# One output copied out of PSUM ungated, and a final norm finished token tile by token tile

## The chip, the cores and the metric

The kernel runs on one core of a Trainium2 chip. The metric is the device time of one execution in microseconds (us); three runs of the kernel before gave a median of 2188.82 us (2184.98 to 2189.14). A core has five engines that run their own instruction streams in order and wait for each other through semaphores: TensorE (PE; PEld is its weight load) multiplies matrices into PSUM, VectorE (DVE), ScalarE (ACT) and GpSimd (POOL) work element by element, and SyncE (SP) issues transfers between device memory and the on-chip SBUF.

## The reference, cut to what matters

One layer of a decoder takes 1024 prompt tokens and 8 x 4 sample tokens (1056 columns here) through two token mixers, retention and latent attention (MLA), and merges them. What the change touches is the end of the layer and the last norm:

```
h_ret  = retention_out(ret_o, rg, ret_gn_w) @ w_down_ret
h_mla  = (mla_o * silu(mg)) @ w_down_mla
merged = sigmoid(ga) * h_ret + sigmoid(gb) * h_mla
x = x + merged @ w_out
x = x + sigmoid(x @ w_ple_gate) * (ple @ w_ple_proj)
y = x * rsqrt(mean(x * x) + eps) * final_norm_w
```

The mean goes over the 1024 features of a token. All data are float32.

## The kernel before, in words

Activations lie transposed: features on the 128 partitions, the 1056 tokens in columns, cut in three thirds of 352. Each float32 product is made of three products of split operands (high by high, low by high, high by low: L266, L267, L268). The helper `gemm` runs the 8 x 3 multiplications of one third into a PSUM buffer `mm`, of which there are two, and calls a function that takes the result out (`evac`). `load_w` brings weights into a raw buffer `wr` (L246), ScalarE casts them to the high part `wh` (L247), VectorE subtracts for the low part `wl` (L199).

The last stage starts at about 1674 us. Its first part makes the gated MLA output: for each of eight output tiles f, the weights of w_down_mla are loaded, the gate logits `gb` come from device memory and get their sigmoid on ScalarE (L1402, L1403), and VectorE multiplies PSUM by the gate while it takes the result out to `M[f]` (L1417). The first tile takes the thirds in the order 2, 0, 1, since the last attention head's last third is ready first. After each tile, a tile of the gated retention output `go` is loaded and split for later (`gl`, L1386; cast `gh`, L1092; VectorE's subtraction, L199). Gate tiles live in three slots (`w4`), so the load of the fourth waits until the first is used up. Then follow w_down_ret (which adds to `M`, 16 tiles), w_out, and the last part.

The last part runs over the three thirds (`third(j, ...)`). In each, eight feature tiles f give a gate product `mm` and a projection `ac`; ScalarE makes the sigmoid (`sg`, L1526), VectorE multiplies by the projection (L1527) and adds `xr`, which GpSimd has put together from its two parts (L1523), into `yT` (L1528). Every two tiles, `turn` transposes `yT` back on TensorE so that tokens lie on partitions (token tiles of 128, 128 and 96 rows; L1502). ScalarE squares and sums the 256 columns into `ss` (L1504, with a read of its accumulator), VectorE multiplies by the norm's weight into `yn` (L1505). After the fourth quarter the norm is finished: VectorE adds the four sums of each of the three token tiles (L1533) and scales them (L233), GpSimd takes the power -1/2 of all three columns at once (L235), ScalarE and VectorE each scale half of the 1024 columns of each tile (L1539, L1540), and SP stores it (L1542; the last 32 rows are the sample tokens, L1544). The end of thirds 0 and 1 is run after the first feature tile of the next third has been issued. The framework orders each engine's instructions by the order of the code and its own estimate of when they are due; each engine runs its own list strictly in order.

## Time and profile before

| what | us |
|---|---|
| three runs, median (lowest to highest) | 2188.82 (2184.98 to 2189.14) |
| the profiled execution, its own time | 2187.65 |
| its span, from the first to the last instruction | 2185.8 |
| TensorE busy in the span | 2138.7 (98%) |
| VectorE busy | 1234.5 (56%) |
| ScalarE busy | 731.1 (33%) |
| GpSimd busy | 317.4 (15%) |

The granted TensorE clock of this execution was 0.995. Profile rows read: start, duration, engine, line of the kernel, operation, output<-input, shapes, count; in square brackets the idle time of the engine before the row and what released it. Rows of waits read: who waited, for whom, total us, times, longest. Rows of groups read: line, engine, operation, shapes, count, then busy us, mean ns of one, and idle time before with its releaser. A busy share is an average over a span whose stages differ, so what counts for an edit is which wait ends last at its place.

### The profile page before, as it was taken

To read this page: it belongs to the slowest core of one execution; us is meant where nothing else is said; L and a number is where in the kernel's file an instruction comes from. 1 tells how busy PE (TensorE), PEld (TensorE's weight loads), DVE (VectorE), ACT (ScalarE), POOL (GpSimd) and SP (SyncE) were. 2 spreads that over 40 slices of the span, in tenths; PEclk is the share of its full clock that TensorE was granted. 3 is DMA by queue.
4 is the path that set the end of the run, shared out by engine and by line. 5 is a ranking of instruction groups with operands and counts; after the bars stand their busy time and mean duration, and the time that the engine had idled before them with its cause. 6 is when DMAs were issued, how large, how long until landed. Compare 5 with 4: busy or idle time off the path is not lost.

```text
span 2185.8 us, 38552 instructions
## 1 busy us (share of the span) xinstructions
PE 2138.7 (98%) x15368; PEld 1858.5 (85%) x15368; DVE 1234.5 (56%) x2776; ACT 731.1 (33%) x1537; POOL 317.4 (15%) x511
## 2 busy tenths in 40 slices
PE   8999999999999999999999999899998999999997
PEld 7997877777777898888788887788887999999997
DVE  5424564565655356656666664778676353444465
ACT  6412322333333222221222311454556342222243
POOL 2211111111110022222121220122221000000121
PEclk9999999999999999999999999999999999999999
DMA  8447666566565321532613517110112353234243
GB/s 239 136 139 263 213 218 230 177 250 216 211 231 178 112 68 49 172 116 88 208 41 121 179 52 252 51 37 12 38 51 73 130 197 98 82 96 124 78 143 115
DMA packets 264356, 299.71 MB, mean 137 GB/s; under 512 B 26544, under 2 KB 221744, under 8 KB 260080
## 3 DMA queue, kind: packets, MB, share of 16 engines
q1 hardware_dynamic: 254960, 213.36, 31.5%
q0 software_dynamic: 9216, 83.89, 10.2%
q8 instruction: 121, 1.98, 0.4%
q14 instruction: 59, 0.48, 0.1%
HBM read 233.03 MB, written 64.17 MB: 136 GB/s over the span
## 4 chain that ended last, share of the span: by engine, by line
PE 61%; issue 4%; DVE 3%; DMA 1%; ACT 1%; POOL 1%; POOLq 0%; ACTq 0%; DVEq 0%; SPq 0%
PE mm L266 15%; PE mm L267 14%; PE mm L268 14%; PE ac L266 2%; PE ac L268 2%; PE ac L267 2%; PE mm L1302 2%; PE tr L1288 1%; PE ac L1245 1%; PE sc L652 1%; PE tr L852 1%; PE x L683 1%; PE ac L874 1%; PE ac L1246 1%; PE ac L1247 1%
## 5 line engine op out<-in xcount | busy, mean ns | idle before, releaser
L266 PE MATMUL mm<-xh,wh 128*128 128x352 f32 x1344 | 458.3, 341 | 1.0 <-ACT gev L413 0.8
L267 PE MATMUL mm<-xl,wh 128*128 128x352 f32 x1344 | 436.5, 325 | 0.0
L268 PE MATMUL mm<-xh,wl 128*128 128x352 f32 x1344 | 435.5, 324 | 0.0
L266 PEld LDWEIGHTS mm<-xh,wh 128*128 128x128 f32 x1344 | 253.1, 188 | 104.2 <-issue 86.5
L267 PEld LDWEIGHTS mm<-xl,wh 128*128 128x128 f32 x1344 | 254.3, 189 | 5.0 <-issue 2.7
L268 PEld LDWEIGHTS mm<-xh,wl 128*128 128x128 f32 x1344 | 253.9, 189 | 1.5 <-issue 1.5
L199 DVE TENSOR_TENSOR wl<-wr,wh 128x512 fp32r<-128x512 f32 (+2 forms) x251 | 168.5, 683 | 133.2 <-ACT wh L247 107.0
L247 ACT CAST wh<-wr 128x512 fp32r<-128x512 f32 x216 | 129.7, 618 | 285.0 <-PE mm L267 219.9
L648 DVE STREAM_TRANSPOSE kt<-craw 128x512 f32<-128x512 f32 x256 | 160.6, 681 | 108.3 <-PE sc L652 73.1
L413 ACT ACTIVATE gev<-mm 128x352 f32<-128x352 f32 x120 | 55.6, 464 | 233.0 <-PE mm L268 151.5
L266 PE MATMUL mm<-mh,wh 128*128 128x352 f32 x384 | 124.4, 324 | 1.8 <-DVE M L1417 1.8
L268 PE MATMUL mm<-mh,wl 128*128 128x352 f32 x384 | 124.3, 324 | 0.0
L268 PE MATMUL mm<-gh,wl 128*128 128x352 f32 x384 | 124.3, 324 | 0.0
L266 PE MATMUL mm<-gh,wh 128*128 128x352 f32 x384 | 124.3, 324 | 0.0
L267 PE MATMUL mm<-ml,wh 128*128 128x352 f32 x384 | 124.2, 324 | 0.0
L267 PE MATMUL mm<-gl,wh 128*128 128x352 f32 x384 | 124.1, 323 | 0.0
L266 PE MATMUL mm<-wv,xh 128*128 128x512 f32 x256 | 103.0, 402 | 0.0
L267 PE MATMUL mm<-wv,xh 128*128 128x512 f32 x256 | 100.9, 394 | 0.0
L268 PE MATMUL mm<-wv,xl 128*128 128x512 f32 x256 | 100.7, 393 | 0.0
L841 ACT ACTIVATE on<-ac,gb,gs 128x512 f32<-128x512 f32 (+1 forms) x36 | 28.0, 778 | 208.5 <-DVE gb L839 208.2
L652 PE MATMUL sc<-kt,q 32*32 32x512 f32 x2560 | 91.5, 600 | 0.0
L1523 POOL TENSOR_TENSOR xr<-x1h,x1l 128x352 f32<-128x352 f32 x24 | 24.4, 1039 | 406.2 <-DVE pT L199 326.1
(384 smaller groups left out, 4563.0 us busy)
## 6 DMA issues: line engine op xcount, KB each, us to landing
wr<-in_w_in_dram SPq DMA_DIRECT2D x144, 256.0 KB, 3.0
st<-in_state_ret_dram SPq DMA_DIRECT2D x32, 512.0 KB, 4.1
out_ret_sample_dram<-st SPq DMA_DIRECT2D x32, 512.0 KB, 3.7
wr<-in_w_ple_gate_dram SPq DMA_DIRECT2D x48, 256.0 KB, 2.7
gt<-gev SPq DMA_DIRECT2D x48, 176.0 KB, 1.8
gl<-go SPq DMA_DIRECT2D x16, 528.0 KB, 7.6
gate<-ga SPq DMA_DIRECT2D x16, 528.0 KB, 3.3
g<-gt SPq DMA_DIRECT2D x32, 256.0 KB, 3.1
```

Of the source, the lines that this page charges most:

```text
L199: dve.tensor_tensor(out=out, in0=src, in1=b32(hi), op=ALU.subtract)
L247: hi_by[0](hi, raw)
L266: pe.matmul(out, wh, xh, start=first, stop=False)
L267: pe.matmul(out, wh, xl, start=False, stop=False)
L268: pe.matmul(out, wl, xh, start=False, stop=last)
L413: act.activation(t, ps, func)
L648: dve.transpose(kt[:, 2 * i + s].rearrange("p (n r) -> p n r", r=32), src)
L652: pe.matmul(sc[32 * v:32 * v + 32, q, :], Q["q4"][qs_, j + v // 2, 2 * (g % 2) + v % 2, :], kt[qs_, v, :], start=n == 0, stop=n == NJ // 2 ...
L683: pe.matmul(pv[32 * v:32 * v + 32, :KL], pT[:, n, 32 * v:32 * v + 32], keys[v % 2][:, 8 * (v // 2) + n, :], start=n == 0, stop=n == 7, til ...
L841: act.activation(on[:n], po, AF.Identity, bias=nb[:n], scale=s[:n])
L1302: pe.matmul(po[:, :256], v[a][w], t[:, x, 256 * a:256 * a + 256], start=j + a + part == 0, stop=False, skip_group_check=True)
L1523: pool.tensor_tensor(out=xr, in0=b32(x1[f][0][:, sl]), in1=b32(x1[f][1][:, sl]), op=ALU.add)
```

## The change

In the first output tile (f = 0), VectorE now copies the product from PSUM to `M[0]` as it is. The gate is loaded and put through its sigmoid afterwards in the program, and GpSimd multiplies the whole 128 x 1056 tile by it in place. The other seven tiles are gated from PSUM as before.

In the last part, the sums of squares of one token tile now stand next to each other in `ss`, and in the fourth quarter each token tile gets its own mean (one VectorE multiply-and-sum over its four numbers with a tile of ones, `fours`) and its own root (one GpSimd power on one column), ahead of its `yn`. Scaling goes in the order of tiles 0, 1, 2 instead of 2, 0, 1, and is shared 448 columns to ScalarE and 576 to VectorE instead of 512 and 512.

```diff
     for f in range(8):
         w = load_w(A["w_down_mla"][0, :, f * P:(f + 1) * P], 8)
-        gb = gate(gbD, f)
         M.append(xs_("M", dt=F32))
         out = M[f]
-        run(gemm(w, ml, lambda j, ps, sl: dve.tensor_tensor(out=out[:, sl], in0=ps, in1=gb[:, sl], op=ALU.mult), 8,
-                 (2, 0, 1) if f == 0 else range(3)))
+        if f == 0:
+            run(gemm(w, ml, lambda j, ps, sl: dve.tensor_copy(out[:, sl], ps), 8, (2, 0, 1)))
+            gb = gate(gbD, f)
+            pool.tensor_tensor(out=out, in0=out, in1=gb, op=ALU.mult)
+        else:
+            gb = gate(gbD, f)
+            run(gemm(w, ml, lambda j, ps, sl: dve.tensor_tensor(out=out[:, sl], in0=ps, in1=gb[:, sl], op=ALU.mult), 8))
         gx.append(load_gated(f, xs_) if f < 7 else gated(f, xs_))
...
         ss = small(pz, "ss", 12, 2)
         pool.memset(ss, 1.0)
+        r = small(pz, "r", 3, 2)
...
                 q = xs_("sq", (P, 256), F32)
-                act.activation(q[:n], px[:n, :256], AF.Square, accum_out=ss[:n, 3 * quarter + i:3 * quarter + i + 1])
+                act.activation(q[:n], px[:n, :256], AF.Square, accum_out=ss[:n, 4 * i + quarter:4 * i + quarter + 1])
+                if quarter == 3:
+                    v, of = (small(pz, name, 4 if name == "of" else 1, 2) for name in ("v", "of"))
+                    dve.tensor_tensor_reduce(out=of, in0=ss[:, 4 * i:4 * i + 4], in1=fours, scale=1.0 / D, scalar=EPS,
+                                             op0=ALU.mult, op1=ALU.add, accum_out=v)
+                    pool.tensor_tensor(out=r[:, i:i + 1], in0=v, in1=nhalf, op=ALU.pow)
                 dve.tensor_tensor(out=yn[:n, hs], in0=px[:n, :256], in1=fnw[:n, hs], op=ALU.mult)
...
         turn(due, 3)
-        sums = small(pz, "sums", 3, 2)
-        dve.tensor_reduce(out=sums, in_=ss.rearrange("p (q i) -> p i q", i=3), axis=AX.X, op=ALU.add)
-        r = rstd_of(pz, sums, P, 1.0 / D, dve, 3)
-        for i in (2, 0, 1):
+        for i in range(3):
             (a, b, m), yn = tiles[i], Y[i]
             n = b - a
             o = xs_("o", (P, D), F32)
-            act.activation(o[:n, :512], yn[:n, :512], AF.Copy, scale=r[:n, i:i + 1])
-            dve.tensor_scalar(o[:n, 512:], yn[:n, 512:], r[:n, i:i + 1], None, op0=ALU.mult)
+            act.activation(o[:n, :448], yn[:n, :448], AF.Copy, scale=r[:n, i:i + 1])
+            dve.tensor_scalar(o[:n, 448:], yn[:n, 448:], r[:n, i:i + 1], None, op0=ALU.mult)
...
+    fours = pz.tile([P, 4], F32, name="fours")
+    pool.memset(fours, 1.0)
```

Below is what stands on the engines' lists, without times. First SP and ScalarE where the last stage begins; a row is a line of the kernel, an instruction, output<-input, the shape and a count. `gb` and `go` are the device memory of gate logits and of the retention output. SP before, up to the fourth gate, and after:

```order
L1402 DMA gate<-gb_82 128x1056
L1402 DMA gate<-gb_83 128x1056
L1402 DMA gate<-gb_84 128x1056
L1386 DMA gl<-go_102 128x1056
L1402 DMA gate<-gb_85 128x1056
L246 DMA wr<-in_w_down_mla_dram 128x4x128 x2
```

```order
L1402 DMA gate<-gb_82 128x1056
L1386 DMA gl<-go_102 128x1056
L1402 DMA gate<-gb_83 128x1056
L1402 DMA gate<-gb_84 128x1056
L246 DMA wr<-in_w_down_mla_dram 128x4x128 x2
L1402 DMA gate<-gb_85 128x1056
```

The first tile of `go` moves ahead of the second and third gates; the next weights move ahead of the fourth gate, which now waits for GpSimd's multiply to free its slot. ScalarE's list follows: its three gh casts stand between the first gate's sigmoid and the next two. VectorE at the same place, as one piece of the difference:

```order
 L199 TENSOR_TENSOR ml<-mla,mh 128x352 x2
-L1417 TENSOR_TENSOR M<-mm,gate 128x352 x2
+L1417 COPY M<-mm 128x352 x2
+L199 TENSOR_TENSOR gl<-gl,gh 128x352 x3
+L1417 COPY M<-mm 128x352
+L199 TENSOR_TENSOR wl<-wr,wh 128x512 x2
+L1422 TENSOR_TENSOR M<-mm,gate 128x352 x2
```

The two first multiplies become copies, and the third copy stands behind all three splits of `gl` (before, behind two of them). Third, VectorE where third 1 ends and third 2 is already under way (`rs_r` and `r` are the roots, `o` the scaled output). Before:

```order
L1540 TENSOR_SCALAR o<-yn,rs_r_22335 96x512
L1540 TENSOR_SCALAR o<-yn,rs_r_22335 128x512 x2
L1527 TENSOR_TENSOR sg<-sg,ac 128x352
L199 TENSOR_TENSOR wl<-wr,wh 128x512
L1528 TENSOR_TENSOR yT<-sg,xr 128x352
L199 TENSOR_TENSOR wl<-wr,wh 128x512
```

After:

```order
L1515 TENSOR_TENSOR yn<-tr,fnw 96x256
L1547 TENSOR_SCALAR o<-yn,r 128x576 x2
L1547 TENSOR_SCALAR o<-yn,r 96x576
L199 TENSOR_TENSOR wl<-wr,wh 128x512
L1537 TENSOR_TENSOR sg<-sg,ac 128x352
L199 TENSOR_TENSOR wl<-wr,wh 128x512
L1538 TENSOR_TENSOR yT<-sg,xr 128x352
```

Both splits of the weights now stand ahead of this `yT`; before, one of them did. At the end of the last third the three reductions, `yn` and scalings come in the same order as here, with nothing behind them.

## The prediction

> **What bounds the kernel now.** I read the page's list of costly groups first, then the waits of TensorE over the last 510 us (from 1676 us, where the last stage begins, to the end), because a change that lies in that stage can only win what TensorE waits for there, and what stands behind TensorE's last instruction.

> ```profile
> L266 PE MATMUL mm<-mh,wh 128*128 128x352 f32 x384 | 124.4, 324 | 1.8 <-DVE M L1417 1.8
> ...
> PE mm L266 <- DVE M L1417: 1.8, 1, 1.8
> PE tr L1502 <- DVE yT L1528: 0.8, 1, 0.8
> ```

> TensorE waits twice in the whole stage: once for a gated output (L1417) and once at the very end for yT. Everything between is TensorE at work without a gap, so other engines matter there only if they become late. The first wait, in order of time over all engines:

> ```profile
> 1677.70 0.96 DVE L199 TENSOR_TENSOR ml<-mla,mh 128x352 fp32r<-128x352 f32 x2 [0.17 <-ACT mh L1092]
> ...
> 1678.08 1.29 SPq L1402 DMA_DIRECT2D gate<-gb  x3
> 1679.41 0.43 SPq L1386 DMA_DIRECT2D gl<-go  x1
> ...
> 1681.74 1.28 ACT L1403 ACT_TABLE_LOAD   x1 [3.68 <-issue]
> 1682.58 0.32 PE L268 MATMUL mm<-mh,wl 128*128 128x352 f32 x1
> 1683.03 2.21 ACT L1403 ACTIVATE gate<-gate 128x1056 f32<-128x1056 f32 x2
> 1684.15 0.96 DVE L1417 TENSOR_TENSOR M<-mm,gate 128x352 f32<-128x352 f32 x2 [5.48 <-ACT gate L1403]
> 1684.72 0.43 PE L266 MATMUL mm<-mh,wh 128*128 128x352 f32 x1 [1.82 <-DVE M L1417]
> 1684.99 0.32 PE L267 MATMUL mm<-ml,wh 128*128 128x352 f32 x1
> ```

> The gate is asked for at 1678.08, its sigmoid starts at 1683.03, and VectorE, idle for 5.48 us, can multiply only at 1684.15. Two PSUM buffers (mm) are full by then, so the third block of columns cannot start.

> The end of the program, and the rate at which its last stores move:

> ```profile
> 2175.13 0.19 ACT L1504 ACTIVATION_READ_ACCUMULATOR sq<-tr 128x1 f32 x1
> 2175.35 1.14 DVE L1505 TENSOR_TENSOR yn<-tr,fnw 128x256 f32<-128x256 f32 x3 [0.33 <-ACT sq L1504]
> ...
> 2176.41 0.15 DVE L1533 TENSOR_REDUCE sums<-ss 128x3 f32<-128x12 f32 x1
> 2176.60 0.17 DVE L233 TENSOR_SCALAR rs_v<-sums 128x3 f32<-128x3 f32 x1
> 2176.85 0.86 POOL L235 TENSOR_TENSOR rs_r<-rs_v,cst 128x3 f32<-128x3 f32 x1 [25.66 <-DVE rs_v L233]
> 2177.74 1.27 DVE L1540 TENSOR_SCALAR o<-yn,rs_r 96x512 f32<-96x512 f32 x3 [0.97 <-POOL rs_r L235]
> 2177.74 1.95 ACT L1539 ACTIVATE o<-yn,rs_r 96x512 f32<-96x512 f32 x3 [1.70 <-POOL rs_r L235]
> 2178.49 0.53 SPq L1542 DMA_DIRECT2D out_y_prompt_dram<-o  x1
> 2179.07 0.58 SPq L1544 DMA_DIRECT2D out_y_sample_dram<-o  x1
> 2179.75 1.02 SPq L1542 DMA_DIRECT2D out_y_prompt_dram<-o  x2
> ```

> Here nothing overlaps: sum, root (0.86 on GpSimd), scaling, store. In the table of stretches the last three columns are clock, DMA share and GB/s:

> ```profile
> 2178.00:2179.50 1.50, 0.00 (x0) 0.00 (x0) 1.02 (x3) 1.50 (x3) 0.00 (x0) 0.50 0.00 0
> 2179.50:2181.00 1.50, 0.00 (x0) 0.00 (x0) 0.00 (x0) 0.19 (x1) 0.00 (x0) 0.50 0.87 178
> 2181.00:2183.90 2.90, 0.00 (x0) 0.00 (x0) 0.00 (x0) 0.00 (x0) 0.00 (x0) 0.50 1.00 404
> 2183.90:2185.80 1.90, 0.00 (x0) 0.00 (x0) 0.00 (x0) 0.00 (x0) 0.00 (x0) 0.50 0.01 2
> ```

> The bytes start 1.0 us after the first store's issue (2178.49 to 2179.50), crawl at 178 GB/s while the 64-row and 32-row stores go first, then run at 404; 1.9 us of completion follow.

> **The change part by part.**

> *First output copied out ungated.* The copy needs only the product in PSUM. For its length I take the multiply's, 0.96/2 = 0.48 us, which reads the same block of PSUM (a bare copy could be shorter; both lie hidden). VectorE is free at 1678.66 (1677.70 + 0.96), so the first copy is done by about 1679.3 and the first buffer is empty 3 us before the third block wants it. TensorE then goes on at the spacing of its neighbours, 0.16 us: its next start is 1682.74 instead of 1684.72, 1.98 us earlier, and the start after it comes at 1682.90 instead of 1684.99. **Term 1: -2.1 us.** The lower bound is 1.8, the wait alone.

> What is moved or added must stay hidden. The transfer of go's first tile and ScalarE's three gh casts now come before the second and third gates, and VectorE's third copy stands behind three gl splits that wait for these casts. Each of the four transfers is 528 KB; the rows below show the casts start at 1686.75, when it was the last of four, so as second of four it lands earlier; at the latest the casts start as they did.

> ```profile
> 1686.75 1.26 ACT L1092 CAST gh<-gl 128x352 fp32r<-128x352 f32 x3 [0.20 <-DMA gl<-go]
> 1688.75 1.14 ACT L247 CAST wh<-wr 128x512 fp32r<-128x512 f32 x2 [0.74 <-PE mm L267]
> 1693.13 1.08 ACT L1403 ACTIVATE gate<-gate 128x1056 f32<-128x1056 f32 x1 [3.23 <-DMA gate<-gb]
> ...
> 1700.39 1.14 ACT L247 CAST wh<-wr 128x512 fp32r<-128x512 f32 x2 [2.85 <-PE mm L267]
> ```

> At that latest the splits end near 1688.6 and the third copy at 1689.1. A block lasts 24 x 0.16 = 3.9 us, so TensorE wants this buffer at 1682.7 + 3.9 + 3.9 = 1690.5. Cover: 1.4 us at worst, price 0.

> The GpSimd multiply is 128x1056, three blocks of the size of xr, whose row (next fence) has three in 3.12 us: 3.1 us, about 1687.3 to 1690.4. Behind it waits the transfer of the fourth gate on SP's queue, and behind that the next go tile and the later weights. That gate's sigmoid ran at 1693.13; its first use is the first block of the fourth output tile. Output tiles follow at 11.64 us (1688.75 to 1700.39), so that is at about 1713. Even 3 us later it is hidden; so are the weights, which ScalarE took at 1700.39 only when TensorE let go of the slot.

> *Root, scaling and store tile by tile, at the two inner boundaries between thirds.* There TensorE already works on the next third:

> ```profile
> 2141.69 3.12 POOL L1523 TENSOR_TENSOR xr<-x1h,x1l 128x352 f32<-128x352 f32 x3
> 2141.76 3.34 DVE L1540 TENSOR_SCALAR o<-yn,rs_r 96x512 f32<-96x512 f32 x3 [0.98 <-POOL rs_r L235]
> ...
> 2145.46 0.68 DVE L199 TENSOR_TENSOR wl<-wr,wh 128x512 fp32r<-128x512 f32 x1
> 2146.06 0.51 DVE L1528 TENSOR_TENSOR yT<-sg,xr 128x352 f32<-128x352 f32 x1
> ...
> 2147.00 0.82 PE L1502 MATMUL tr<-cst,yT 128*128 128x128 f32 x6
> ```

> This yT ends at 2146.57 and is transposed at 2147.00: 0.43 us of slack. The scalings take 3.34 us beside GpSimd's xr, and 1.27 alone at the end of the program. In the changed order they start sooner (no sums, no wait for one root: 2141.25 by the steps of the next part, 0.5 earlier), but are 576 columns wide instead of 512 (3.34 x 576/512 = 3.76, 0.4 longer), and one weight split (0.60 to the next start) stands before this yT that stood behind it. The net is 0.5 us later against 0.43 of slack: a stall of 0.1 at each boundary, between 0 (the first scaling runs before xr starts) and 0.4 (the new reductions at their upper price). **Term 2: +0.2 us** (0 to 0.8).

> [...]

> *The same step at the end.* The new reduction exists nowhere in the trace; its nearest kin are the masked maximum of the attention, its read of the accumulator, and the root on one column:

> ```profile
> L1253 DVE DVE_READ_ACCUMULATOR2_ANT mx<- 128x1 f32 x26 | 3.6, 140 | 0.0
> L1253 DVE CUSTOM_DVE_ANT_0 ac<-ac,above 128x256 f32<-128x256 f32 x3 | 1.3, 426 | 0.0
> L1253 DVE CUSTOM_DVE_ANT_0 ac<-ac,above 128x128 f32<-128x128 f32 x4 | 1.2, 300 | 0.0
> ...
> L235 POOL TENSOR_TENSOR rs_r<-rs_v,cst 128x1 f32<-128x1 f32 x18 | 9.7, 551 | 1.0
> ```

> From 256 to 128 columns the time falls 0.126 us, so four columns are about 0.18; with the read, and starts that overlap, I take 0.2 us each, and 0.44 (0.30 + 0.14) as the upper bound. VectorE from 2175.35: three reductions and three yn (1.14/3 = 0.35 to the next start) end at 2175.35 + 0.6 + 1.05 = 2177.0; the first scaling (1.27/3 = 0.42, a little more for 576 columns) is done at 2177.5. ScalarE's half is earlier: statistic at 2175.65, root 0.55, so about 2176.3, and 448 columns at some 0.62 (1.95/3 = 0.65 for 512) end by 2176.95. The first store is issued at 2177.54 instead of 2178.49: 0.95 us sooner; the others are ready at 2177.95 and 2178.4, one per SP issue (0.5). The bytes then run without the pause between issues that the 178 GB/s contain. **Term 3: -1.0 us**, between -0.2 (reductions at 0.44: VectorE 0.72 later) and -1.7 (from 2178.55 all 1.44 MB at 404 GB/s, 3.57 us, so to 2182.1 instead of 2183.85).

> [...]

> **The sum**, on the profiled execution (2187.65 us: span 2185.8 and 1.85 around it): 2187.65 - 2.1 + 0.2 - 1.0 = **2184.8 us**, 0.13% less. That execution lies 1.2 under the median of the runs, 2188.82, and inside their spread of 2184.98 to 2189.14.

> **Rivals.**

> A. *VectorE is locked out at the boundaries.* If the scalings cannot start until all three xr are over (2141.5 + 3.1 = 2144.6), and then take 3 x 0.48 = 1.4, yT follows after two splits and the gate product (0.6 + 0.43 + 0.6 + 0.5) at 2148.2, 1.2 us after TensorE asks for it; twice, that is 2.4: 2184.6 + 2.4 = 2187.0. For it: three scalings cost 3.34 against 1.27. Against it: they ended with the third xr (2145.10 and 2144.81), not 1.4 after it, and now the first starts ahead of xr. Chance 0.18.

> B. *The first stall returns one block later*, behind the casts that wait for go's transfer: decisive only from 1.4 us beyond the latest start worked out above. If it takes all of term 1 back: 2184.8 + 2.1 = 2186.9. It is also the result if the copy does not free PSUM sooner. Chance 0.08.

> C. *The stores gain their upper bound and the boundaries cost nothing*: 2187.65 - 2.1 - 1.7 = 2183.9, or 2183 if the narrow stores overlap besides. Chance 0.10.

> D. *Slower.* Three roots at a boundary queue one behind another on GpSimd with VectorE's reductions between them; ScalarE stands in order behind each, so the weight cast and the gate after it come late and TensorE waits. It decides from 1.5 us lost at each boundary beyond the slack (1.5 x 2 eats terms 1 and 3). At 2.0 each: 2184.6 + 4.0 = 2188.6. For it: ScalarE already waits 2.48 us for the root there. Against it: one-column roots take 0.55, three of them 1.65, under that same wait plus slack. Chance 0.06.

> **How the numbers follow.** The forecast has 0.58: 2184.8, on its own between 2183.5 and 2186.5 by the bounds of terms 2 and 3. Two tenths of a per cent, 4.4 us, is about what a measurement of this kernel can tell from no change. The forecast's 2.9 us lies inside that; C and the faster edge of the forecast, with the runs' spread, reach beyond it. Faster 0.27, same 0.67, slower 0.06. A and D pull the upper end to 2188.4, C and the spread the lower to 2182.0.

> **What would show it.** The list of TensorE's waits should lose M and keep yT at the end; a new wait of L1507 on yT near 2104 and 2145, beyond 0.4 us, is A or D; one on the copy near 1690 is B. The stores should begin about 3 us earlier on the span's clock, 128 rows first. I am wrong on term 3 if the first store is issued later than 2.4 us after ScalarE's first accumulator read of the last turn (2175.13 to 2177.54), and on term 1 if TensorE pauses anywhere between the first and the second output tile.

## The result, and the profile after

Eleven runs of the changed kernel have a median of 2181.50 us (2178.04 to 2185.42), eleven of the kernel before 2189.14 (2184.98 to 2196.56): a ratio of 0.9971, 95% interval 0.9961 to 0.9981. The change made the kernel faster by 0.3%. The profiled execution took 2180.01 us (span 2178.2, granted clock 0.998), 7.6 us less than the profiled one of before. The forecast was 2184.8 with a range down to 2182.0. The median lies 0.5 us below that range, the profiled execution 2.0. Of the runs told of further down, one, a twelfth of kernel e3, took 11735.3 us and is in no mean.

**Where the 7.6 us come from.** TensorE's list has the same order in both programs, so the start times of the same instruction in the two traces can be subtracted. The profile after was already 3.84 us ahead at the first gate's issue (1678.08 before, 1674.24 after), ahead of anything the change touches. It was 5.92 ahead at the second output tile, 5.88 behind both inner boundaries, and 7.56 at the end. So the change itself brings 2.1 + 0.0 + 1.7, together 3.7 us of this pair, and the other half has another source.

The waits of TensorE after the change, from 1672 us to the end; the row of M is gone:

```profile
PE tr L1507 <- DVE yT L1538: 0.8, 1, 0.8
```

The other engines around the first output tile, in order of time:

```profile
1674.24 0.34 SPq L1402 DMA_DIRECT2D gate<-gb  x1
1674.64 0.42 SPq L1386 DMA_DIRECT2D gl<-go  x1
1675.28 0.53 DVE L1417 COPY M<-mm 128x352 f32<-128x352 f32 x1 [0.45 <-PE mm L268]
1679.10 0.53 DVE L1417 COPY M<-mm 128x352 f32<-128x352 f32 x1 [3.30 <-PE mm L268]
1680.42 1.24 ACT L1092 CAST gh<-gl 128x352 fp32r<-128x352 f32 x3
1680.92 1.40 DVE L199 TENSOR_TENSOR gl<-gl,gh 128x352 fp32r<-128x352 f32 x3 [1.29 <-ACT gh L1092]
1683.00 0.53 DVE L1417 COPY M<-mm 128x352 f32<-128x352 f32 x1 [0.68 <-PE mm L268]
1683.67 2.48 POOL L1419 TENSOR_TENSOR M<-M,gate 128x1056 f32<-128x1056 f32 x1 [9.50 <-ACT gate L1403]
1684.17 3.13 DVE L199 TENSOR_TENSOR wl<-wr,wh 128x512 fp32r<-128x512 f32 x2 [0.65 <-ACT wh L247]
1694.04 1.09 ACT L1403 ACTIVATE gate<-gate 128x1056 f32<-128x1056 f32 x1 [9.38 <-DMA gate<-gb]
```

All three copies now wait for TensorE, none for a gate. GpSimd's multiply lies where nobody waits for it, and the fourth gate comes late without harm.

One inner boundary:

```profile
2092.35 2.15 POOL L1514 TENSOR_TENSOR r<-v,cst 128x1 f32<-128x1 f32 x3 [19.28 <-DVE v L1512]
2093.37 2.22 DVE L1547 TENSOR_SCALAR o<-yn,r 128x576 f32<-128x576 f32 x3
2094.30 5.98 POOL L1533 TENSOR_TENSOR xr<-x1h,x1l 128x352 f32<-128x352 f32 x5
...
2095.76 1.19 DVE L199 TENSOR_TENSOR wl<-wr,wh 128x512 fp32r<-128x512 f32 x1 [0.16 <-ACT wh L247]
...
2098.23 1.26 DVE L1538 TENSOR_TENSOR yT<-sg,xr 128x352 f32<-128x352 f32 x1
...
2099.70 0.82 PE L1507 MATMUL tr<-cst,yT 128*128 128x128 f32 x6
```

The first two scalings (0.51 and 0.52 us) are over or nearly so when GpSimd's xr begins; yT ends at 2099.49, 0.21 us before TensorE takes it. The other boundary has the same durations within 0.02 us on VectorE. The single rows also show what VectorE's instructions took beside GpSimd's, on which the forecast and rival A differ. The third scaling, the two splits and yT each begin while a piece of xr runs, and end 0.3 to 0.6 us after that piece ends (xr 2094.30 to 2095.28, scaling 2094.54 to 2095.59; xr 2097.71 to 2099.11, yT 2098.23 to 2099.49). The scaling took 1.05 us there, against 0.51 and 0.52 for the two ahead of it, and yT 1.26, against 0.52 where no xr ran (2091.68). The gate product between the splits took 0.51 us inside a piece (2096.87 to 2097.38). No row lasts through all of xr; why some take longer and this one does not was not tried.

And the end of the program, with the stretches of its stores (last two columns: DMA share, GB/s):

```profile
2169.33 0.19 ACT L1509 ACTIVATION_READ_ACCUMULATOR sq<-tr 128x1 f32 x1
...
2169.55 0.16 DVE L1512 CUSTOM_DVE_ANT_0 of<-ss,fours 128x4 f32<-128x4 f32 x1 [0.33 <-ACT sq L1509]
...
2169.64 0.42 DVE L1515 TENSOR_TENSOR yn<-tr,fnw 128x256 f32<-128x256 f32 x1
...
2169.80 2.14 POOL L1514 TENSOR_TENSOR r<-v,cst 128x1 f32<-128x1 f32 x3 [24.46 <-DVE v L1512]
...
2170.39 0.67 ACT L1546 ACTIVATE o<-yn,r 128x448 f32<-128x448 f32 x1
...
2170.81 1.69 DVE L1547 TENSOR_SCALAR o<-yn,r 128x576 f32<-128x576 f32 x3
2171.39 1.26 ACT L1546 ACTIVATE o<-yn,r 128x448 f32<-128x448 f32 x2 [0.34 <-POOL r L1514]
2171.39 1.82 SPq L1549 DMA_DIRECT2D out_y_prompt_dram<-o  x3
2173.26 0.99 SPq L1551 DMA_DIRECT2D out_y_sample_dram<-o  x1
```

```profile
2172.00:2174.73 2.73, 0.00 (x0) 0.00 (x0) 0.50 (x1) 0.65 (x2) 0.00 (x0) 0.51 0.93 377
2174.73:2176.40 1.67, 0.00 (x0) 0.00 (x0) 0.00 (x0) 0.00 (x0) 0.00 (x0) 0.50 0.94 248
2176.40:2178.20 1.80, 0.00 (x0) 0.00 (x0) 0.00 (x0) 0.00 (x0) 0.00 (x0) 0.50 0.00 0
```

The first store goes out 2.06 us after ScalarE's first accumulator read (3.36 before). The bytes start fast, at 377 GB/s, and the narrow stores come last, in the stretch at 248.

**The other half of the pair.** Of the 3.84 us upstream, 3.1 arise between 743 and 753 us. In the stretches of before and then of after, the clock is the third number from the end:

```profile
745.00:750.00 5.00, 5.00 (x25) 5.00 (x25) 1.02 (x2) 0.00 (x0) 2.58 (x14) 0.59 0.26 65
750.00:755.00 5.00, 5.00 (x25) 5.00 (x24) 0.00 (x0) 0.84 (x2) 0.46 (x4) 0.72 0.60 240
```

```profile
745.00:750.00 5.00, 5.00 (x37) 5.00 (x37) 1.02 (x2) 0.00 (x0) 3.03 (x16) 1.00 0.36 107
750.00:755.00 5.00, 5.00 (x33) 5.00 (x32) 0.69 (x1) 1.53 (x3) 0.00 (x0) 1.00 0.96 332
```

TensorE was granted half its clock from 745.94 to 752.76 us in the profile before, and ran 25 matmuls in 5 us instead of 37 and 33. A suspect stands just ahead, a run of 32 narrow matmuls (32 columns each) at the end of the page attention; f2, g1 and g2 further down try it. In before:

```profile
743.01 4.19 PE L741 MATMUL x<-out,wv 128*128 128x32 f32 x32
```

Three theories were tried. **1**: the change's own effect is about 3.9 us; the rest is half-clock stretches that come and go. **2**: any change of the program shifts these stretches. **3**: all 7.6 us belong to the change.

### The profile page after: what moved, and what is told of

Same layout as the page of the kernel before. It is cut to its first block, busy times and chain, and to the rows that moved or that the text cites. A ratio compares the mean times of both kernels' runs of the same rounds, so it can differ in the third digit from the quotient of the medians.

```text
span 2178.2 us, 38580 instructions
## 1 busy us (share of the span) xinstructions
PE 2135.6 (98%) x15368; PEld 1856.0 (85%) x15368; DVE 1237.5 (57%) x2788; ACT 729.6 (33%) x1537; POOL 324.5 (15%) x519
## 3 DMA queue, kind: packets, MB, share of 16 engines
q8 instruction: 121, 1.98, 0.4%
## 4 chain that ended last, share of the span: by engine, by line
PE 62%; DVE 3%; issue 3%; DMA 1%; ACT 1%; POOL 1%; SPq 0%; ACTq 0%; POOLq 0%; DVEq 0%
PE mm L266 15%; PE mm L267 15%; PE mm L268 15%; PE ac L266 2%; PE ac L268 2%; PE ac L267 2%; PE mm L1302 2%; PE tr L1288 1%; PE sc L652 1%; PE tr L852 1%; PE ac L1245 1%; PE x L683 1%; PE ac L874 1%; PE ac L1246 1%; PE ac L1247 1%
## 5 line engine op out<-in xcount | busy, mean ns | idle before, releaser
L266 PE MATMUL mm<-xh,wh 128*128 128x352 f32 x1344 | 457.1, 340 | 0.9 <-ACT gev L413 0.7
L267 PE MATMUL mm<-xl,wh 128*128 128x352 f32 x1344 | 435.4, 324 | 0.0
L268 PE MATMUL mm<-xh,wl 128*128 128x352 f32 x1344 | 434.4, 324 | 0.0
L266 PEld LDWEIGHTS mm<-xh,wh 128*128 128x128 f32 x1344 | 252.2, 188 | 104.1 <-issue 86.5
L267 PEld LDWEIGHTS mm<-xl,wh 128*128 128x128 f32 x1344 | 253.3, 188 | 4.9 <-issue 2.7
L268 PEld LDWEIGHTS mm<-xh,wl 128*128 128x128 f32 x1344 | 253.1, 188 | 1.5 <-issue 1.5
L199 DVE TENSOR_TENSOR wl<-wr,wh 128x512 fp32r<-128x512 f32 (+2 forms) x251 | 172.2, 698 | 129.7 <-ACT wh L247 103.6
L247 ACT CAST wh<-wr 128x512 fp32r<-128x512 f32 x216 | 129.7, 618 | 277.6 <-PE mm L267 225.1
L268 PE MATMUL mm<-gh,wl 128*128 128x352 f32 x384 | 124.3, 324 | 0.0
L268 PE MATMUL mm<-mh,wl 128*128 128x352 f32 x384 | 124.3, 324 | 0.0
L266 PE MATMUL mm<-mh,wh 128*128 128x352 f32 x384 | 124.3, 324 | 0.0
L266 PE MATMUL mm<-gh,wh 128*128 128x352 f32 x384 | 124.2, 324 | 0.0
L267 PE MATMUL mm<-ml,wh 128*128 128x352 f32 x384 | 124.2, 324 | 0.0
L267 PE MATMUL mm<-gl,wh 128*128 128x352 f32 x384 | 124.2, 323 | 0.0
L266 PE MATMUL mm<-wv,xh 128*128 128x512 f32 x256 | 103.0, 402 | 0.0
L267 PE MATMUL mm<-wv,xh 128*128 128x512 f32 x256 | 100.9, 394 | 0.0
L268 PE MATMUL mm<-wv,xl 128*128 128x512 f32 x256 | 100.7, 393 | 0.0
L1533 POOL TENSOR_TENSOR xr<-x1h,x1l 128x352 f32<-128x352 f32 x24 | 26.9, 1145 | 389.9 <-DVE pT L199 311.6
```

What stands on the lines that cost most here:

```text
L199: dve.tensor_tensor(out=out, in0=src, in1=b32(hi), op=ALU.subtract)
L247: hi_by[0](hi, raw)
L266: pe.matmul(out, wh, xh, start=first, stop=False)
L267: pe.matmul(out, wh, xl, start=False, stop=False)
L268: pe.matmul(out, wl, xh, start=False, stop=last)
L1533: pool.tensor_tensor(out=xr, in0=b32(x1[f][0][:, sl]), in1=b32(x1[f][1][:, sl]), op=ALU.add)
```

## The experiments

The runs of each of three groups share a chip and the runs of the kernel before on it. There the medians of the kernel before are 2177.45 to 2178.0, some 11 us less than in the first comparison; between the profiles of before and of e1, 7.8 of this difference arise between 305 and 727 us, in the page attention, far from the change. Means are over the runs; the error behind each is the standard error.

| kernel | runs | mean us | ratio to before (95%) |
|---|---|---|---|
| before, group e | 35 | 2177.76 ± 0.35 | |
| e1, unused tile | 11 | 2177.10 ± 0.49 | 0.9996 (0.9988 to 1.0005) |
| e2, first part | 11 | 2176.28 ± 0.54 | 0.9990 (0.9981 to 0.9999) |
| e3, second part | 11 | 2175.35 ± 0.60 | 0.9989 (0.9980 to 0.9998) |
| e4, in effect the change again | 11 | 2173.79 ± 0.45 | 0.9981 (0.9972 to 0.9990) |
| before, group f | 23 | 2178.37 ± 0.56 | |
| f1, the change again | 12 | 2173.82 ± 0.70 | 0.9981 (0.9971 to 0.9991) |
| f2, change, narrow run spread | 12 | 2171.93 ± 0.55 | 0.9974 (0.9965 to 0.9984) |
| before, group g | 16 | 2178.45 ± 0.49 | |
| g1, before, narrow run spread | 11 | 2175.20 ± 0.49 | 0.9985 (0.9976 to 0.9994) |
| g2, change, narrow run spread | 6 | 2171.74 ± 0.52 | 0.9970 (0.9958 to 0.9983) |

### e1: an unused tile

```diff
+    fours = pz.tile([P, 4], F32, name="fours")
+    pool.memset(fours, 1.0)
```

> The kernel before with one unused 128x4 tile and its memset on GpSimd, which the change also brings, and nothing else of it. Theory 1 (own effect 3.9 us; the other 3.7 of the profiled pair is a half-clock stretch behind the 32 narrow matmuls at 743 us, whose appearance is luck): time as before, 2187 to 2190, some runs 3 us lower; the profile may or may not show the stretch at 746-753. Theory 2 (any change of the program shifts the clock): 2185 or less without any of the change, clock 0.997 or 0.998 in nearly all runs. Theory 3 (all 7.6 us are the change's own): 2189, as before.

The time is that of before within its interval. Its profile has a half-clock stretch of one window (3.41 us) behind the narrow matmuls, and the first profile of the change none. So this change of the program, at least, moves nothing that can be measured, and nothing speaks for theory 2.

### e2 and e3: the two parts apart

e2 has the diff of the output tile alone, e3 that of the norm alone (with `fours`).

> The first part alone: the first output copied out ungated, gated by GpSimd later; the norm as before. Theory 1: 2.1 us below the kernel before at the same clock (1.8 if the boundary savings belong to the other part), all of it between the starts of the first output's last matmul group and the next group, near 1684. Theory 3: about half of 7.6 us.

> The second part alone: root, scaling and store by token tile, gates as before. Theory 1: 1.8 us below the kernel before at the same clock, all of it behind the last accumulator read (first store 1.3 us sooner, end 1.8 sooner). Forecast on record: 0.8 us. Theory 3: the rest of 7.6 us.

By the means, e2 takes 1.5 ± 0.6 and e3 2.4 ± 0.7 us less than before, together 3.9. The traces are sharper than the means. From the last narrow attention product (the last matmul of L1302/L1307) to the 200th matmul behind it, TensorE took 34.41, 34.48 and 34.06 us in three profiles that gate from PSUM (before, e1, and g1 below), and 32.30 to 32.44 in nine that copy (32.68 in a tenth, g2): 1.4 to 2.2 us less, **2.1 in the first pair**, as forecast (in g1 TensorE's wait for M is 1.5 us instead of 1.8 or more). From the start of the last wide matmul to the end the profiles with the old norm took 12.74 to 12.77 us (before, e1, e2, g1), those with the new norm 10.98 to 11.03 (after, e3, e4, f1, f2, g2): **1.75 us**, where the forecast had 1.0.

e3 held a surprise. Here TensorE still waits for M, and this wait, too, was followed by half the clock, so that the same 200 matmuls took 35.99 us:

```profile
1672.87 0.43 PE L266 MATMUL mm<-mh,wh 128*128 128x352 f32 x1 [1.86 <-DVE M L1417]
...
1673.97 0.49 PE L266 MATMUL mm<-mh,wh 128*128 128x352 f32 x1
```

```profile
1670.00:1673.00 3.00, 1.14 (x8) 0.85 (x7) 0.71 (x2) 2.99 (x3) 0.00 (x0) 1.00 1.01 411
1673.00:1677.00 4.00, 4.00 (x17) 4.00 (x18) 1.21 (x3) 2.35 (x5) 0.00 (x0) 0.61 0.02 7
```

That is 1.5 us which the change saves now and then on top of its 2.1: in one of the four profiles that gate from PSUM.

### e4 and f1: the change again

e4 was to break up the narrow run by steps of a supply of wide work that, as TensorE's list then showed, is used up before this place:

```diff
                 pe.matmul(po[:, h * NR:(h + 1) * NR], wv[:, c, h, :], olT[:, c, h].rearrange("p b t -> p (b t)"), start=c == 0, stop=c == 1)
+            if h % 2 == 1 and h < HM - 1:
+                next(fill, None)
+                next(fill, None)
```

> The changed kernel, with the run of 32 narrow matmuls (128x32) at 743 us broken up: after each two heads two of the wide matmul steps that otherwise follow are put in, so no stretch of narrow matmuls is longer than 0.5 us. Theory 1: no half-clock stretch near 746-753 in any run; time of the changed kernel's runs that have none there (2178 to 2181), and less spread between runs. If the narrow matmuls have nothing to do with the clock: times and spread as the changed kernel (2178 to 2185).

> The changed kernel as it is, beside the kernel before on one chip. Theory 1 (own effect 3.9 us: 2.1 at the first output, 1.8 behind the last accumulator read; the rest of the first pair's 7.6 is half-clock stretches that come and go): 3.5 to 4.2 us below before by the mean, whatever the level of the chip. Theory 3 (7.6 us are its own): 7 to 8 us below.

The order of instructions did not change, so e4 is the changed kernel once more; that expectation is void, and e4, like f1, measures the change once more, on another chip than f1. Both give 0.9981; by the means 4.0 and 4.5 us less. Neither interval reaches 7.6 us (the lower ends are 6.1 and 6.3 us). Theory 3 falls there. Both profiles do have a half-clock stretch behind the narrow run.

### f2, g1 and g2: the narrow run broken up

```diff
+    rest = gate_tiles(C_MG, mgD, range(4, 5), AF.Silu)
...
             for c in range(2):
                 pe.matmul(po[:, h * NR:(h + 1) * NR], wv[:, c, h, :], olT[:, c, h].rearrange("p b t -> p (b t)"), start=c == 0, stop=c == 1)
+            if h % 2 == 1 and h < HM - 1:
+                next(rest, None)
+                next(rest, None)
...
-    run(gate_tiles(C_MG, mgD, range(4, 5), AF.Silu))
+    run(rest)
```

> The changed kernel, with the narrow matmuls (128x32) at about 740 us broken into four groups and two wide steps (six matmuls) between the groups, taken from the 88 of the next gate tile, so that the same work is done in another order. If the narrow run causes the half-clock stretch there: none near 736-753 in its profile, mean 0.5 to 1.5 us below the changed kernel on this chip, and a smaller spread. If not: as the changed kernel.

> The kernel before with its narrow matmuls at about 743 us broken into four groups with wide steps between them. Theory 1: no half-clock stretch near 746-753; mean 1 to 2.5 us below the kernel before, as much as the same edit gave the changed kernel.

> The changed kernel with the same edit, beside the one above on the same chip: with the narrow run out of the way in both, the change's own effect. Theory 1: 3.5 to 4.2 us below the run above. Theory 3 (7.6 us are the change's own): 7 to 8 us below.

None of the three profiles has half the clock there; of the eleven with the run in one piece, seven have it. One line of stretches from f1 and one from f2, the same change on one chip:

```profile
740.00:745.00 5.00, 5.00 (x24) 5.00 (x23) 0.80 (x2) 0.00 (x0) 3.00 (x16) 0.69 0.66 234
```

```profile
738.00:743.00 5.00, 5.00 (x38) 5.00 (x37) 1.74 (x3) 1.51 (x3) 1.91 (x7) 1.00 0.24 63
```

f2 gains 1.5 us on f1 at this place.

One profile of each kernel is little, but the granted clock of every run of these groups is on record, and it says the same. It averages 0.9959 in the sixteen runs of before in group g, and 0.9974 in the eleven of g1; f1 has 0.9970, f2 and g2 0.9975. One window at half clock takes 0.0008 off it (half of 3.41 us in 2175), so by this estimate g1 has lost 1.8 ± 0.4 such windows in a run, about 2.8 us.

With the run spread in both, the change is worth 2175.20 - 2171.74 = 3.5 ± 0.7 us. The edit itself gave before 3.2 ± 0.7 us, where 1 to 2.5 was expected, and the change 1.9 ± 0.9, where it was 0.5 to 1.5. f2 gains another 2.2 us on f1 between 890 and 1090 us of their profiles, in the retention. Most of it is a wait for the loaded state, in f1 and in f2:

```profile
PE ac L1021 <- DMA st<-in_state_ret_dram: 2.2, 3, 1.2
```

```profile
PE ac L1026 <- DMA st<-in_state_ret_dram: 0.3, 1, 0.3
```

After and e1, with the run in one piece, waited 0.8 and 1.2 us there, g1 and g2 0.2 and 0.5. Why the loads come earlier behind the spread run was not tried. f2 and g2 are the fastest kernels of this study, 0.26% and 0.30% under before; f2 lies 1.9 ± 0.9 us under the change on its chip.

### f3, f4, g3 and g4: what the norm's 1.75 us are made of

f3 puts the joint root back and keeps store order and split; f4 is the same kernel once more; g3 is f3 with the old order; g4 is the change with the old split.

```diff
-                if quarter == 3:
-                    v, of = (small(pz, name, 4 if name == "of" else 1, 2) for name in ("v", "of"))
...
+        sums = small(pz, "sums", 3, 2)
+        dve.tensor_reduce(out=sums, in_=ss.rearrange("p (i q) -> p i q", q=4), axis=AX.X, op=ALU.add)
+        r = rstd_of(pz, sums, P, 1.0 / D, dve, 3)
-        for i in range(3):
+        for i in (2, 0, 1):
```

The last pair of lines is in g3 alone; g4 has 512 for 448 in the two scaling lines.

> The changed kernel with the three reductions and roots of each third made together again as before; the store order (0, 1, 2) and the 448/576 split stay. Time from the last wide matmul to the end (before 12.77, 12.74 and 12.75 us in three profiles; changed 11.03, 10.98, 10.99): forecast's view, in which the root per tile makes the first store 0.95 us sooner and no more: 11.9 to 12.0. If the order of the stores brings 0.45 us by itself: 12.2 to 12.3 for this one, less the part that the root per tile gave.

> The same kernel once more, for the spread of the time from the last wide matmul to the end: within 0.05 us of the run before.

> The changed kernel with the joint root and the store order (2, 0, 1) of before, the 448/576 split kept. From the last wide matmul to the end (joint root with order 0, 1, 2: 12.23 and 12.26; before 12.75): 12.7 if the store order makes the remaining 0.5 us, 12.25 if it is the split.

> The changed kernel with the columns split 512/512 between ScalarE and VectorE as before; roots by tile, order (0, 1, 2). From the last wide matmul to the end (changed: 10.98 to 11.03): 11.0 to 11.1 if the order makes the remaining 0.5 us, 11.4 to 11.5 if it is the split.

| us from the start of the last wide matmul | first store issued | end |
|---|---|---|
| old norm (before, e1, e2, g1) | 5.47 to 5.48 | 12.74 to 12.77 |
| g3: joint root, order 2, 0, 1, split 448 | 5.43 | 12.71 |
| f3, f4: joint root, order 0, 1, 2, split 448 | 5.43, 5.44 | 12.23, 12.26 |
| g4: root by tile, order 0, 1, 2, split 512 | 4.16 | 10.96 |
| root by tile, order 0, 1, 2, split 448 (after, e3, e4, f1, f2, g2) | 4.18 to 4.19 | 10.98 to 11.03 |

The two runs of the joint root (f3, f4) agree within 0.04. The root by tile is worth 1.24 us, all of it as an earlier first store. The order of the stores is worth 0.47 (g3 against the mean of f3 and f4) with the first store at the same time; what it is worth with the root by tile was not tried, but the two add up to the 1.75. The split is worth nothing that shows. The bytes of f3 and then of g3 show how the order pays:

```profile
2170.17:2172.67 2.50, 0.00 (x0) 0.00 (x0) 0.00 (x0) 0.29 (x1) 0.00 (x0) 0.50 1.01 406
2172.67:2174.67 2.00, 0.00 (x0) 0.00 (x0) 0.00 (x0) 0.00 (x0) 0.00 (x0) 0.50 0.80 213
```

```profile
2164.70:2166.70 2.00, 0.00 (x0) 0.00 (x0) 0.00 (x0) 0.30 (x1) 0.00 (x0) 0.53 0.79 188
2166.70:2169.70 3.00, 0.00 (x0) 0.00 (x0) 0.00 (x0) 0.00 (x0) 0.00 (x0) 0.50 0.87 355
```

The stretch with the narrow stores (64 and 32 rows) is the slower one in either place, at 213 GB/s in f3 and 188 in g3. In g3 they go first, each alone until SP has issued the next (in before, with the same order, these two issues took 0.53 and 0.58 us), and the wide ones follow at 355 GB/s; in f3 everything is queued by the time they run. This reading of the two rates is argued; the 0.47 us is measured.

## Why the prediction was right or wrong

**The bound** was read right: TensorE, and two waits in the last stage. The first is gone in every profile of a kernel that copies.

**Term 1, -2.1 us: right**, 2.1 measured, and by the forecast's steps. The copies took 0.53 us (0.48 estimated). The third ended 1.7 us ahead of the forecast's latest case (1683.53, which is 1687.4 on the clock of before, against 1689.1) and waited for TensorE alone, because go's tile had landed by 1680.42. GpSimd's multiply took 2.48 us where 3.1 was estimated; the fourth gate's sigmoid waited for its transfer until 1694.04 and cost nothing. Nothing in the trace shows rival B.

**Term 2, +0.2 us: 0.0.** The step that failed is that the scalings start 0.5 us sooner and take 3.76 us. They started 1.1 us sooner (2093.37; 2100.36 before, less the 5.9 by which this profile was ahead) and took 2.22, since most of them ran ahead of xr: the lower bound that the forecast named, and not its choice. The contention went to what came next (a weight split at 1.19 us, yT at 1.26 instead of 0.51), and yT still had 0.21 us to spare. TensorE waits at neither boundary, so rivals A and D did not come. Rival A needs a scaling that waits for all three pieces of xr; in the rows the third scaling ends 0.31 us behind the first piece, ahead of the end of the second (2096.40).

**Term 3, -1.0 us: -1.75, mis-sized in two steps.** First, the price of a reduction: 0.2 us each was taken, but the three pairs of reduction and yn took 1.26 us (2169.55 to 2170.81) where three yn alone would take 1.05, so 0.07 each: the next instruction starts before the reduction and its read are over (the first yn at 2169.64, the reduction's end at 2169.71, its read's at 2169.72). That makes the first store 1.29 us sooner instead of 0.95. Second, the forecast kept 1.0 against its own row-based bound of 1.7, as if the order of the stores were worth nothing. That was the author's estimate, and no run shows it: the order is worth 0.47 us (g3 against f3 and f4). The stretch with the narrow stores is slow in f3 too, 213 GB/s against 406 with the wide ones; what the estimate left out is the place in the queue, and how that works is only argued above. The sum that was right, 2187.65 - 2.1 - 1.7 = 2183.9, stands in the prediction as rival C with a chance of 0.10: the own effect of the change is 3.7 us in the first pair of traces (2.1 and 1.75 by its two parts), 4.0 and 4.5 by the means on two other chips, 3.5 with the narrow run spread.

**What no term held.** 3.1 us of the first pair are the half-clock stretch that the profile before had at 746 us and the one after did not. The change does not remove it: e4 and f1, the same program as after, have such a stretch in their profiles. As far as the change goes, this part of the gain is luck. The forecast took the profiled execution as the kernel's time and its clock of 0.995 as given; it did not ask which stretches made up that number and whether the next execution would have them. Two windows make 3.1 us, as much as the whole forecast gain, and with them the time fell below the range and the likeliest case, no change that can be measured, did not come. That case also rested on 4.4 us as the least that can be told from no change; with eleven runs each the interval was ± 0.1%, some 2 us, and the 4.0 and 4.5 us of e4 and f1 are clear of no change too.

**What stays open.** In the first comparison the medians of eleven runs each differ by 7.6 us; in the later ones the change gave 3.5 to 4.5. The interval of the first reaches down to 4.2 us. The clock of the changed kernel's runs there averages 0.9975, against 0.9968 in e4 and 0.9970 in f1: by the estimate above some 0.7 window less at half clock, or 1 us. Of the other runs of before in the first comparison no clock is known, so whether they mostly had the stretch, as the profiled one did, or something else in those runs adds to the gain, cannot be told from here.

## What to carry to other kernels

An execution's granted clock belongs to its sum: find each half-clock stretch in the trace of before and say what an execution without it would take, before a gain of the same size is forecast from one pair. A wait of TensorE can cost more than its length, and taking it away can gain more than the wait: in one of the four profiles that gate from PSUM (e3), the 1.86 us were followed by half the clock, 1.5 us on top of them. At the end of a program, what finishes first should leave first (1.24 us here), with wide stores ahead of narrow ones (0.47 us here).

## What the runs showed of the hardware

```profile
PE ac L1245 <- ACT pr L1263: 2.9, 1, 2.9
```

| stretch | profile: share | half clock |
|---|---|---|
| narrow run, about 3.5 us | f1 and g4 0.97, f4 0.96, e4 0.95, e1 0.94, f3 0.88, before 0.86 | yes |
| narrow run | e2 0.76, e3 and g3 0.73, after 0.68 | no |
| wait in the attention, about 2.95 us | f2 and f3 0.86, e2 0.79, after 0.74, e1 0.73, e3 and f1 0.70, before and g1 0.63, e4 0.58 | yes |
| wait in the attention | g4 0.53, g2 0.49, g3 0.48, f4 0.43 | no |
| wait for M, 1.5 to 1.9 us | e3 0.54 | yes |
| wait for M | before 0.50, e1 and g1 0.43 | no |

Of the waits in this table, half the clock followed each with a share of 0.54 (e3) or more, and none with 0.53 (g4) or less. Of the narrow runs, whose matmuls the profile shows as busy without a gap, it followed each with 0.86 (before) or more, and none with 0.76 (e2) or less. Of some 8800 windows up to the last matmul in the fourteen profiles, counting idle times over 0.05 us, none outside the table has a share above 0.53 (in before and after none above 0.44), and full clock turned into half behind none with less than 0.54. The window in which the last matmul of before ends is idle for 0.47, the time behind that matmul included, and half the clock followed it too. One window at half clock costs 1.5 us here (matmuls at 0.293 us spacing instead of 0.162). Behind a window at half clock that was itself idle or narrow for 0.25 or more, the clock stayed at half (before 0.31, and f3, e4); behind one with 0.17 or less it was full again (f1, e1). So half the clock followed a wait of 1.86 us that lay in one window (e3), and did not follow one of about 2.95 us with 0.49 in its fullest window (g2).
